# One pool of five PSUM banks in place of turns over pools of three and two, in a two-layer mixer trunk

## The chip, the cores and the metric

The kernel runs on one core of a Trainium2 chip. The metric is the device time of one launch in microseconds, as the median of three runs. Beside it stands one execution recorded by the hardware profiler; every duration below comes from that execution.

## What is computed

The reference runs two layers over 128 context tokens and 512 latent tokens that share all weights (model width 1024). Each layer is a half SwiGLU network, a token mixer, and a second half SwiGLU network:

```python
def trunk_layer(x, cond, lp, ssd_s0, ret_s0, ctx_kv):
    mod = (jax.nn.silu(cond) @ lp['w_mod'] + lp['b_mod'])[:, None, :]
...
    x = x + 0.5 * g1 * swiglu(modulate(rmsnorm(x, nw[0]), sh1, sc1), lp['ffn_w_in'][0], lp['ffn_w_out'][0])
    y, s_ssd, s_ret, k, v = token_mixing(modulate(rmsnorm(x, nw[1]), sh2, sc2), lp, ssd_s0, ret_s0, ctx_kv)
    x = x + g2 * y
    x = x + 0.5 * g3 * swiglu(modulate(rmsnorm(x, nw[2]), sh3, sc3), lp['ffn_w_in'][1], lp['ffn_w_out'][1])
```

Token mixing multiplies by one input matrix, gives the columns to four mixers (a state-space scan "ssd", a long convolution "hyena", a retention scan and a windowed attention), and multiplies what they return by one output matrix. The scans and the attention work in chunks of 128 tokens: five chunks, of which the first is the context. The hidden width of the SwiGLU networks is 2816.

## The kernel before

The 640 tokens are columns, held as two groups of 320. A large fp32 product is made of three TensorE products, of a high and a low part of each operand (`hh` and `hl` of the activations, `hi` and `lo` of the weights): high times high, high times low, low times high. In the rows these are `mm<-hh,hi`, `mm<-hh,lo` and `mm<-hl,hi`. They are called **large products** here. They use three PSUM banks (pool `mmp`, tile `mm`), and VectorE (DVE) or ScalarE (ACT) empties a bank when its sum is complete: gates of the mixers go through ACT (`u<-mm,ucg`), the mixers' output product is added to the residual on DVE (`x<-mm,gate,x`, in `accumulate`).

All the mixers' **small products** (scores, values, states, transposes by the identity `ident`) go through `mx()`, which hands out one bank of a second set of five. Before the change `mx()` counts its calls modulo five: turns 0 to 2 take a bank of pool `mxp` (three banks), turns 3 and 4 one of pool `xtp` (two banks). The turn belongs to the place of the call in the program text.

The second SwiGLU network of each layer (`ffn7`) replaces eight quarter products by seven (`quad`); there `mx()` keeps to the three banks (`self.wide = False`), and two of the results, `mb` and `mc`, take the two banks of `xtp`.

The engines work through their own instructions in order. That order isn't the one of the text: a scheduler lays the instructions of all streams out when the program is built, and takes an instruction when its engine and its tiles' buffers are free by its own reckoning. So large products of work that doesn't depend on a mixer are laid between that mixer's small ones, and which bank a tile waits for decides where. During a mixer the large products are those of the next mixer's inputs; the program's order of mixers is hyena, ssd, attention, retention, then the output product (`mix_out`).

In the attention (`attention`), for each chunk `scores` makes for each of four heads a tile `big` of up to 512 columns (two products: `mx<-u,u` and `mx<-ckT,u`) and, for chunks 1 to 3, a tile `right` of 128 columns, which DVE masks and reduces into `sc` (with the running maximum `amx`). ACT then takes the exponentials. `values` transposes `sc` on TensorE (`mx<-ident,sc`), copies to `pT`, and multiplies by the values (`mx<-u,pT`, `mx<-cv,pT`). In the retention (`retention`), `out1` of a chunk makes four score products (`mx<-u,u`, masked to `M`), for chunks after the first eight products with the states (`mx<-inc,u`, `mx<-st,u`), and four with the values (`mx<-u,M`); DVE and ACT normalise the result `y`, and `out2` transposes it one chunk later (`mx<-ident,y`) for `mix_out`. A small fp32 product stands in the trace with two instructions, a transpose with one.

A small product with `64*128` in its row of the trace contracts the 64 channels of a head, and its operands lie in partitions 0 to 63 or 64 to 127 (in the attention the lower half for heads 0 and 1, the upper for heads 2 and 3); the large products and the transposes contract 128.

The part of `scores` in which the tiles are asked for:

```python
                for h in range(4):
...
                    big = self.mx(512)
...
                    if hi > 512:
                        right = self.mx(128)
```

Of the kernel before, what the change touches and what calls it, by code (L numbers as in the profile page):

```python
# [10 lines left out]
F32 = mybir.dt.float32  # L11
# [4 lines left out]
PSUM = bass.MemoryType.PSUM  # L16
# [37 lines left out]
class Trunk:  # L54
# [38 lines left out]
        self.nc.tensor.transpose(out, in_, self.ident[b : b + n, b : b + n])  # L93

    def mx(self, *shape):

        self.turn = (self.turn + 1) % 5
        if self.wide and self.turn >= 3:
            t = self.xtp.tile([128, 512], F32, tag="xt", name="mx")
        else:  # L100
            t = self.mxp.tile([128, 512], F32, tag="mx", name="mx")
        return self.shaped(t, shape)

    @staticmethod
# [23 lines left out]
    def setup(self):  # L128
        tc, nc, ctx, I = self.tc, self.nc, self.ctx, self.I
        pool = lambda name, bufs=1, **k: ctx.enter_context(tc.tile_pool(name=name, bufs=bufs, **k))  # L130
        self.cp = cp = pool("const")
        self.sp = pool("small", 2)
        self.wp = pool("w", 3)
        self.ringp = pool("ring", NB)
        self.mmp = pool("mmp", 3, space=PSUM)
        self.xtp = pool("xtp", 2, space=PSUM)
        self.mxp = pool("mxp", 3, space=PSUM)
        self.turn, self.wide = 0, True
        self.ssum, self.V = {}, {}
        self.drp = pool("dr", 1, space=bass.MemoryType.DRAM)  # L140

        self.ident = cp.tile([128, 128], F32, name="ident")
        make_identity(nc, self.ident)
        self.ones = cp.tile([128, 128], F32, name="ones")
        nc.gpsimd.memset(self.ones, 1.0)
        self.mhalf = cp.tile([128, 8], F32, name="mhalf")
        nc.gpsimd.memset(self.mhalf, -0.5)
        self.sel = cp.tile([128, 2], F32, name="sel")
        self.dma(self.sel, I["sel"])
        cond = cp.tile([128, 8, 2], F32, name="cond")  # L150
        self.dma(cond, I["cond"])
        self.cs = self.ring("cs")[:, :256].rearrange("p (a b) -> p a b", a=8)
        nc.gpsimd.memset(self.cs, 0.0)
        self.act(self.cs[:, :, 0:2], cond, AF.Silu)
        self.par = []
        for li in range(NL):
            t = cp.tile([128, PC.n], F32, name=f"par{li}")
            self.dma(t, I["par"][li])
            self.par.append(t)
        self.xnew()  # L160

        self.hw = [[cp.tile([128, 8, 322 if g == 0 else 320], F32R, name=f"h{p}{g}") for g in range(2)] for p in "hl"]
        self.hh, self.hl = ([[self.hw[p][g][:, m, 0:320] for g in range(2)] for m in range(8)] for p in range(2))
        self.mod = [cp.tile([128, 72, 2], F32, name=f"mod{li}") for li in range(NL)]
        self.sc = [cp.tile([128, 3, 8, 2], F32, name=f"sc{li}") for li in range(NL)]
        self.gate = [cp.tile([128, 3, 8, 2], F32, name=f"gate{li}") for li in range(NL)]
# [326 lines left out]
    def quad(self, li, w, f, sp, mp, halves):  # L493

        nc = self.nc
        gate, up = (self.rawload(self.I["ffnin"][li, w, 2 * f + i], 1024) for i in range(2))
        a11, a12, a21, a22 = gate[:, :512], gate[:, 512:], up[:, :512], up[:, 512:]
        sa = sp.tile([128, 2, 512], F32, tag="sa", name="sa", bufs=1)  # L500
        sb = sp.tile([128, 2, 512], F32, tag="sb", name="sb", bufs=SB)
        add = self.tt
        ab = self.wsplit(gate)
        add(sa[:, 0], a21, a11, SUB)
        add(sb[:, 0], a21, a22, ADD)
        add(sa[:, 1], sb[:, 0], a11, SUB)
        add(sb[:, 1], a12, sa[:, 1], SUB)
        new = lambda pool, tag, name: pool.tile([128, 512], F32, tag=tag, name=name)[:, :320]
        A, B, C = new(self.mmp, "mm", "mm"), new(self.xtp, "xt", "mb"), new(self.xtp, "xt", "mc")
        sg = mp.tile([128, 640], F32, tag="sg", name="sg", bufs=2)  # L510

        def copied(ps, name):
            t = mp.tile([128, 320], F32, tag="cp", name=name, bufs=CB)
            self.acopy(t, ps)
            return t

        self.product(B, ab, 1, "B21", True, True)
        self.product(A, ab, 0, "B11", True, False)
        p1 = copied(A, "p1")
        self.tt(sg[:, :320], B, p1, ADD)  # L520
        self.act(sg[:, :320], sg[:, :320], AF.Silu)
        wa = self.wsplit(sa.rearrange("p a b -> p (a b)"))
        self.product(C, wa, 0, "T3", True, False)
        p7 = copied(C, "p7")
        yield
        w4 = self.wsplit(a22)
        self.product(A, wa, 1, "T2", False, False)
        q = copied(A, "q")
        self.product(C, w4, 0, "T4", False, True)
        self.tt(q, C, q, ADD)  # L530
        self.tt(sg[:, :320], q, sg[:, :320], MUL)
        gh = self.ring("gh", 640, F32R)
        gl = self.ring("gl", 640, F32R)
        if halves:
            self.split(gh[:, :320], gl[:, :320], sg[:, :320])
        yield
        wb = self.wsplit(sb.rearrange("p a b -> p (a b)"))
        self.product(A, wb, 0, "T1", False, False)
        self.tt(p7, A, p7, ADD)
        yield  # L540
        self.product(A, wb, 1, "B22", False, True)
        self.act(sg[:, 320:], A, AF.Silu)
        self.tt(sg[:, 320:], p7, sg[:, 320:], MUL)
        o = 320 if halves else 0
        self.split(gh[:, o:], gl[:, o:], sg[:, o:])
        self.G.append([(gh[:, 320 * g : 320 * g + 320], gl[:, 320 * g : 320 * g + 320]) for g in range(2)])

    def ffn7(self, li, w, todo, rate, after_group):
        I, n = self.I, 2 * w
        pool = lambda name: self.tc.tile_pool(name=name, bufs=2, side="right", reuse_waits="tile")  # L550
        with pool("ws") as sp, pool("ffn") as mp, pool("mods") as modp, self.tmp():
            self.wide = False
            mods = self.modulation(todo, modp, bufs=MBUF, pin=PIN) if todo else iter(())
            credit = 0.0
            self.G = []
# [76 lines left out]
                done = after_group(g)  # L632
                next(done, None)
            next(done, None)
            self.wide = True


    def sin(self, pool, a, ps, b, fr):
# [522 lines left out]
    def attention(self, li, UQ, UK, UV):  # L1161
        nc, I, O, pm = self.nc, self.I, self.O, self.par[li]
        Y = UQ
        with self.tc.tile_pool(name="att", bufs=1, side=SIDES["att"], reuse_waits="tile") as p:
# [53 lines left out]
            def scores(c):  # L1218
# [33 lines left out]
                if hi > 512:  # L1252
                    self.tt(mx, mx, mx2, MAX)
                self.tt(mx, mx, pm[:, PC.sink], MAX)
                neg = self.small([128, 4], "aneg")
                self.ts(neg, mx, -1.0, MUL)
                es = self.small([128, 4], "aes")
                self.tt(es, pm[:, PC.sink], neg, ADD)
# [398 lines left out]
```

## Time and profile before

| what | value |
| --- | --- |
| runs | 2802.38, 2803.92, 2805.83 us; median 2803.92 us |
| the profiled execution | 2796.57 us, of which the span from the first to the last instruction is 2794.8 us |
| TensorE (PE) busy | 2708.9 us, 97% of the span |
| VectorE (DVE) busy | 1921.8 us, 69% |
| ScalarE (ACT) busy | 1001.2 us, 36% |
| mean granted TensorE clock | 0.987 of full speed |

The profiled execution lies 7.35 us under the median of the runs. A busy engine is one with an instruction under way; on PE a busy microsecond can still be a slow one, as the granted clock of a stretch shows. An idle stretch on PE is named in the rows with the instruction that ended it.

### The profile page before, as it was taken

How to read it: one execution, taken by the hardware profiler on the slowest of the kernel's cores; microseconds unless marked ns; L12 is line 12 of the kernel's file. 1: busy time of each engine (PE TensorE's matmuls, PEld its weight loads, DVE VectorE, ACT ScalarE, POOL GpSimd, SP SyncE). 2: the span in 40 equal slices, each digit the busy share in tenths (PEclk: the TensorE clock that was granted, in tenths of full speed). 3: DMA queues.
4: the chain of work that ended last, by engine and by line, in shares of the span. 5: the costliest groups of instructions: out<-in, count | busy, mean ns of one | idle time of the engine just before them, and what ended most of it. 6: DMA issues, size and time to landing. Idle time of an engine off the chain costs nothing.

```text
span 2794.8 us, 45752 instructions
## 1 busy us (share of the span) xinstructions
PE 2708.9 (97%) x17990; PEld 2601.4 (93%) x17990; DVE 1921.8 (69%) x4040; ACT 1001.2 (36%) x2047; POOL 115.6 (4%) x191
## 2 busy tenths in 40 slices
PE   5999999999999999999999999999999999999999
PEld 3899999999889899999989999998999888999999
DVE  5867677666765688766677676676568467766666
ACT  3222222332544353333442223223336434334432
POOL 0000000100010200000020000002001002000000
PEclk9999999999999999999999999999999999999999
DMA  7454544421213123222235444443213021222222
GB/s 265 145 183 144 159 143 162 136 81 63 80 51 99 52 76 117 85 86 76 82 138 181 146 144 137 143 155 99 80 57 101 18 72 59 83 81 72 83 73 94
DMA packets 121169, 300.52 MB, mean 108 GB/s; under 512 B 20062, under 2 KB 44974, under 8 KB 120572
## 3 DMA queue, kind: packets, MB, share of 16 engines
q1 hardware_dynamic: 120956, 297.61, 33.1%
q8 instruction: 142, 2.33, 0.3%
q14 instruction: 71, 0.58, 0.1%
HBM read 283.36 MB, written 14.20 MB: 106 GB/s over the span
## 4 chain that ended last, share of the span: by engine, by line
PE 89%; DVE 5%; POOL 1%; issue 1%; ACT 1%; DMA 1%; SPq 0%; POOLq 0%; ACTq 0%; DVEq 0%
PE mm L88 70%; PE mx L88 10%; PE mc L88 5%; PE mb L88 3%; PE mx L93 2%; DVE lo L61 1%; DVE x L70 1%; POOL nsum L294 1%; ACT hi L76 0%; DMA E<-cumd 0%; DVE wmj L278 0%; DVE hl L61 0%; DVE nx L70 0%; DVE gl L61 0%; POOL nrs L125 0%
## 5 line engine op out<-in xcount | busy, mean ns | idle before, releaser
L88 PE MATMUL mm<-hh,hi 128*128 128x320 f32 (+2 forms) x3136 | 993.0, 317 | 9.1 <-ACT hh L76 4.0
L88 PE MATMUL mm<-hh,lo 128*128 128x320 f32 (+2 forms) x3136 | 989.5, 316 | 7.7 <-DVE lo L61 7.7
L88 PE MATMUL mm<-hl,hi 128*128 128x320 f32 (+2 forms) x3136 | 990.4, 316 | 2.1 <-DVE hl L61 2.1
L76 ACT CAST hi<-raw 128x1024 fp32r<-128x1024 f32 (+4 forms) x406 | 346.0, 852 | 858.1 <-PE mm L88 809.4
L88 PEld LDWEIGHTS mm<-hh,hi 128*128 128x128 f32 (+1 forms) x3136 | 596.6, 190 | 19.3 <-ACT hh L76 5.6
L88 PEld LDWEIGHTS mm<-hh,lo 128*128 128x128 f32 (+1 forms) x3136 | 598.9, 191 | 16.0 <-DVE lo L61 8.4
L88 PEld LDWEIGHTS mm<-hl,hi 128*128 128x128 f32 (+1 forms) x3136 | 597.1, 190 | 13.5 <-issue 5.6
L61 DVE TENSOR_TENSOR lo<-raw,hi 128x1024 fp32r<-128x1024 f32 (+4 forms) x406 | 395.5, 974 | 183.0 <-ACT hi L76 182.0
L88 PE MATMUL mm<-gh,hi 128*128 128x320 f32 x1408 | 437.5, 311 | 7.2 <-DVE x L70 6.7
L88 PE MATMUL mm<-gl,hi 128*128 128x320 f32 x1408 | 435.2, 309 | 1.8 <-DVE gl L61 1.4
L88 PE MATMUL mm<-gh,lo 128*128 128x320 f32 x1408 | 434.5, 309 | 0.0
L70 DVE SCALAR_TENSOR_TENSOR x<-mm,gate,x 128x128 f32<-128x128 f32 (+2 forms) x624 | 253.8, 434 | 181.1 <-PE mm L88 178.6
L278 DVE CUSTOM_DVE_ANT_0 wmj<-wm,condb 128x1024 bf16<-128x1024 f32 x264 | 321.2, 1217 | 2.4 <-ACT condb L73 1.2
L88 PEld LDWEIGHTS mm<-gh,hi 128*128 128x128 f32 x1408 | 264.3, 188 | 13.6 <-PE mm L88 9.7
L88 PEld LDWEIGHTS mm<-gl,hi 128*128 128x128 f32 x1408 | 264.4, 188 | 5.8 <-DVE gl L61 4.4
L88 PEld LDWEIGHTS mm<-gh,lo 128*128 128x128 f32 x1408 | 264.5, 188 | 0.0
L70 DVE SCALAR_TENSOR_TENSOR gu<-mm,cg,sg 128x128 f32<-128x128 f32 x132 | 54.2, 436 | 157.7 <-ACT cg L76 103.6
L294 POOL TENSOR_TENSOR nsum<-nsum,nsq 128x320 f32<-128x320 f32 x60 | 54.2, 904 | 1384.3 <-ACT nsq L73 946.6
L88 PE MATMUL mc<-th,lo 128*128 128x320 f32 x320 | 98.7, 309 | 0.1
L88 PE MATMUL mc<-th,hi 128*128 128x320 f32 x320 | 98.7, 308 | 0.0
L88 PE MATMUL mc<-tl,hi 128*128 128x320 f32 x320 | 98.6, 308 | 0.0
L76 ACT COPY cg<-mm 128x2 f32<-128x2 f32 x88 | 14.1, 160 | 213.6 <-PE mm L88 213.2
(283 smaller groups left out, 3247.6 us busy)
## 6 DMA issues: line engine op xcount, KB each, us to landing
raw<-in_ffnin SPq DMA_DIRECT2D x176, 512.0 KB, 3.5
wm<-in_wmodT SPq DMA_DIRECT2D x132, 512.0 KB, 3.6
raw<-in_mixin SPq DMA_DIRECT2D x52, 512.0 KB, 3.4
raw<-in_ffnoutA SPq DMA_DIRECT2D x80, 256.0 KB, 2.6
raw<-in_ffnoutA SPq DMA_DIRECT2D x48, 320.0 KB, 2.8
wms<-in_wmod SPq DMA_DIRECT2D x12, 512.0 KB, 3.4
raw<-in_ffnoutB SPq DMA_DIRECT2D x12, 512.0 KB, 3.4
raw<-in_mixout SPq DMA_DIRECT2D x16, 384.0 KB, 3.0
```

Source lines behind the costliest of these rows:

```text
L61: self.nc.vector.tensor_tensor(out, a, b, op=op)
L70: self.nc.vector.scalar_tensor_tensor(out, a, s, b, op0=op0, op1=op1)
L76: self.nc.scalar.copy(out, in_)
L88: return self.nc.tensor.matmul(out, lhsT=lhsT, rhs=rhs, start=start, stop=stop, **k)
L93: self.nc.tensor.transpose(out, in_, self.ident[b : b + n, b : b + n])
L278: return self.nc.vector.tensor_tensor_reduce(junk, raw, cb, 1.0, 0.0, op0=MUL, op1=ADD, accum_out=out)
L294: (adder or (self.nc.vector if g and m > 5 else self.nc.gpsimd)).tensor_tensor(s, s, sq, op=ADD)
```

## The change

`xtp` is taken away and `mxp` has five banks; `mx()` always takes the next bank of `mxp`, and so do `mb` and `mc`. The count of turns and the switch `wide` are gone. No arithmetic changes.

```diff
     def mx(self, *shape):
-
-        self.turn = (self.turn + 1) % 5
-        if self.wide and self.turn >= 3:
-            t = self.xtp.tile([128, 512], F32, tag="xt", name="mx")
-        else:
-            t = self.mxp.tile([128, 512], F32, tag="mx", name="mx")
+        t = self.mxp.tile([128, 512], F32, tag="mx", name="mx")
         return self.shaped(t, shape)
...
         self.mmp = pool("mmp", 3, space=PSUM)
-        self.xtp = pool("xtp", 2, space=PSUM)
-        self.mxp = pool("mxp", 3, space=PSUM)
-        self.turn, self.wide = 0, True
+        self.mxp = pool("mxp", 5, space=PSUM)
...
-        A, B, C = new(self.mmp, "mm", "mm"), new(self.xtp, "xt", "mb"), new(self.xtp, "xt", "mc")
+        A, B, C = new(self.mmp, "mm", "mm"), new(self.mxp, "mx", "mb"), new(self.mxp, "mx", "mc")
...
-            self.wide = False
...
-            self.wide = True
```

The scheduler lays out another order with it. TensorE's instructions are the same ones in both programs and stand in the same order in the SwiGLU networks; they stand elsewhere in the mixers of both layers, and a few at the start and around the norms. Three places follow, all of the first layer; the second layer's mixers show the same patterns.

First place, on TensorE (PE): the attention's scores of chunk 2. `u_7613` and `u_7610` are the keys, `u_7489`, `u_7551` and `u_7486`, `u_7548` the queries, `ckT` the cached keys. Before:

```order
L88 MATMUL mx<-u_7613,u_7489 128x256
L88 MATMUL mx<-ckT,u_7489 128x256
L88 MATMUL mm<-hh_106,lo 128x322
L88 MATMUL mm<-hh_106,hi 128x322
L88 MATMUL mx<-u_7613,u_7489 128x128
L88 MATMUL mx<-u_7613,u_7551 128x256
L88 MATMUL mx<-ckT,u_7551 128x256
L88 MATMUL mx<-u_7613,u_7551 128x128
L88 MATMUL mm<-hl_108,hi 128x322
```

And now:

```order
L88 MATMUL mx<-u_7610,u_7486 128x256
L88 MATMUL mx<-ckT,u_7486 128x256
L88 MATMUL mx<-u_7610,u_7486 128x128
L88 MATMUL mx<-u_7610,u_7548 128x256
L88 MATMUL mx<-ckT,u_7548 128x256
L88 MATMUL mx<-u_7610,u_7548 128x128
L93 MATMUL mx<-ident,sc 128x128 x4
L88 MATMUL mm<-hh_103,lo 128x322
```

The scores of a chunk (two such halves, eight tiles for chunks 1 to 3) now stand together, with transposes of the exponentials of the chunk before right behind them and no large product between; the large products follow in blocks of 2 to 23.

Second place, on TensorE: the end of the retention, from the last chunk's products with the values (`mx<-u,M`) to the transposes of the last two chunks of `y`; the large products are those of `mix_out`. Before:

```order
L88 MATMUL mx<-u_8615,M 128x64 x2
L88 MATMUL mx<-u_8677,M 128x64 x2
L93 MATMUL mx<-ident,y 128x128 x2
L88 MATMUL mm<-hh_107,hi 128x320
L88 MATMUL mm<-hl_109,hi 128x320
```

And now:

```order
L88 MATMUL mx<-u_8674,M 128x64 x2
L88 MATMUL mm<-hh_104,hi 128x320
L88 MATMUL mm<-hl_106,hi 128x320
L88 MATMUL mm<-hh_104,lo 128x320
...
L93 MATMUL mx<-ident,y 128x128 x2
L88 MATMUL mm<-hh_103,hi 128x320
```

Between the last `mx<-u,M` and the last but one `mx<-ident,y` there stand 12 large products now and none before (13 now in the second layer); between the two last `mx<-ident,y` 29 now and 14 before (36 and 14 in the second layer). They come from the blocks that stood between attention and retention (119 large products in the first layer, 81 in the second; 8 now in each) and behind the retention. Within the retention the products of one chunk stand together now, with 12 to 16 large ones to the next transposes.

Third place, on ScalarE (ACT): the end of the attention, where the retention's gate (`u_8736<-mm,ucg`, a silu) meets the last chunk's exponentials (`sc,asum<-sc,aneg`). Before, one load behind the whole attention served that gate. Now:

```order
L76 COPY ucg<-mm 128x2
L73 ACT_TABLE_LOAD
L73 ACTIVATE u_8736<-mm,ucg 128x128
...
L73 ACTIVATE u_8736<-mm,ucg 128x192
L76 COPY pT<-mx 128x128
L73 ACT_TABLE_LOAD
L73 ACTIVATE sc,asum<-sc,aneg 128x512 x4
L73 ACTIVATE aes<-aes 128x4
...
L73 ACT_TABLE_LOAD
L73 ACTIVATE u_8736<-mm,ucg 128x320
```

The gate's first half is now ahead of the exponentials and its second half behind them, so the function tables change three times where they changed once; over the program there are 13 table loads instead of 9, two more in each layer.

## Rows read from the trace of the kernel before

**Rows 1.** The page: span, and TensorE's busy time.

```profile
span 2794.8 us, 45752 instructions
...
PE 2708.9 (97%) x17990; PEld 2601.4 (93%) x17990; DVE 1921.8 (69%) x4040; ACT 1001.2 (36%) x2047; POOL 115.6 (4%) x191
```

**Rows 2.** The page: shares of the chain that ended last, by engine.

```profile
PE 89%; DVE 5%; POOL 1%; issue 1%; ACT 1%; DMA 1%; SPq 0%; POOLq 0%; ACTq 0%; DVEq 0%
```

**Rows 3.** The page: costliest groups, results of the seven products on TensorE.

```profile
L88 PE MATMUL mc<-th,hi 128*128 128x320 f32 x320 | 98.7, 308 | 0.0
```

**Rows 4.** Timeline of TensorE, end of retention: start, length, instruction, [idle before, releaser].

```profile
914.83 1.00 PE L88 MATMUL mx<-u,M 128*128 128x64 f32 x8
916.84 0.41 PE L93 MATMUL mx<-ident,y 128*128 128x128 f32 x2 [1.01 <-DVE y L61]
918.92 0.63 PE L88 MATMUL mm<-hh,hi 128*128 128x320 f32 x1 [1.66 <-DVE x L70]
...
2289.18 0.41 PE L93 MATMUL mx<-ident,y 128*128 128x128 f32 x2 [1.37 <-DVE y L61]
2291.25 0.63 PE L88 MATMUL mm<-hh,hi 128*128 128x320 f32 x1 [1.67 <-DVE x L70]
```

**Rows 5.** Timeline of DVE there, first layer.

```profile
916.27 0.43 DVE L61 TENSOR_TENSOR y<-y,rrr 128x256 f32<-128x256 f32 x1
...
916.95 0.34 DVE L70 SCALAR_TENSOR_TENSOR x<-mm,gate,x 128x128 f32<-128x128 f32 x1
...
918.46 0.87 DVE L70 SCALAR_TENSOR_TENSOR x<-mm,gate,x 128x192 f32<-128x192 f32 x2
```

**Rows 6.** Stretches (us): length, PE busy (instructions), granted clock, DMA share, GB/s.

```profile
2266.00:2273.00 7.00, 7.00 (x32) 0.52 0.01 2
...
918.90:924.90 6.00, 5.98 (x23) 0.50 0.20 66
924.90:930.00 5.10, 5.10 (x36) 1.00 0.32 103
...
2291.20:2297.10 5.90, 5.85 (x22) 0.51 0.19 51
```

**Rows 7.** The chain in order of time, first layer's ssd: start, length, what.

```profile
752.35 3.00 DMA E<-cumd
...
758.94 1.34 PE mx L88 x10
```

**Rows 8.** Waits of TensorE, 600 to 1000 us: total, times, longest.

```profile
PE mx L88 <- DVE E L61: 2.4, 1, 2.4
...
PE mx L88 <- DVE amx L1245: 0.3, 1, 0.3
```

**Rows 9.** Timeline of TensorE, first layer's attention, first scores of chunk 2.

```profile
812.94 0.70 PE L88 MATMUL mx<-u,u 64*128 64x256 f32 x2
813.48 0.38 PE L88 MATMUL mx<-ckT,u 64*128 64x256 f32 x1
813.53 0.48 PE L88 MATMUL mx<-u,u 64*128 64x256 f32 x1
```

**Rows 10.** The same timeline, the rest of three heads and large products around it.

```profile
814.59 0.41 PE L88 MATMUL mm<-hh,lo 128*128 128x322 f32 x1
814.84 0.31 PE L88 MATMUL mm<-hh,hi 128*128 128x322 f32 x1
815.08 0.92 PE L88 MATMUL mx<-u,u 64*128 64x128 f32 x4
...
816.58 0.41 PE L88 MATMUL mm<-hl,hi 128*128 128x322 f32 x1
816.83 0.31 PE L88 MATMUL mm<-hh,lo 128*128 128x322 f32 x1
816.98 0.31 PE L88 MATMUL mm<-hh,hi 128*128 128x322 f32 x1
```

**Rows 11.** Timeline of DVE there: the reductions of two successive heads.

```profile
814.11 0.69 DVE L1245 CUSTOM_DVE_ANT_0 sc<-mx,amask 128x512 f32<-128x512 f32 x1 [0.53 <-PE mx L88]
...
814.93 0.69 DVE L1245 CUSTOM_DVE_ANT_0 sc<-mx,amask 128x512 f32<-128x512 f32 x1
```

**Rows 12.** Timeline of ACT behind the attention: a table load and what follows.

```profile
865.47 1.28 ACT L73 ACT_TABLE_LOAD   x1
866.77 1.91 ACT L73 ACTIVATE condb<-condb 128x2048 f32<-128x2048 f32 x1
```

**Rows 13.** Timeline of DVE, retention: the same reduction of two successive chunks.

```profile
914.39 0.42 DVE L1138 TENSOR_REDUCE rvs<-vt 128x4 f32<-128x256 f32 x1
...
919.24 0.41 DVE L1138 TENSOR_REDUCE rvs<-vt 128x4 f32<-128x256 f32 x1
```

## The prediction

> **What bounds the kernel now.** I read the page first: TensorE is busy for 2708.9 of 2794.8 us [rows 1], and the chain that ended last runs over it for 89% [rows 2]. So what counts is TensorE's 86 us of idle time and its slow time; VectorE and ScalarE matter only where TensorE waits for them. The seven-product results have no wait ahead of them (0.0 us before `mc`, in 320 products [rows 3]), and their order stays, so I cost what the change does to `mb` and `mc` at nothing. Then I went through TensorE's timeline in both layers' mixers, looking for idle stretches and for the granted clock behind them.
>
> Three things are to be seen there. First, the end of the retention: when its last `mx<-u,M` is done (914.83 plus 1.00) there is no large product to do; TensorE stands 1.01 us for `y`, then 1.66 us for the additions to `x` that free the banks of the large products. The second layer does the same with 1.37 and 1.67 us [rows 4]. VectorE shows why: the addition at 916.95 stands behind the scaling of `y` at 916.27, and the next two only at 918.46 [rows 5]. Second, right behind either stall TensorE runs at half clock for some 6 us: 23 instructions fill 5.98 us there, while 36 fill 5.10 us in the stretch after it [rows 6]. Third, in the first layer's ssd the decay tile `E` is fetched by a 3.00 us transfer on the chain, and TensorE waits 2.4 us for what VectorE makes of it [rows 7, 8].
>
> **The change, part by part.** The arithmetic, TensorE's instructions and the number of banks stay. What changes is the order in which TensorE gets its small products, and four table loads on ScalarE.
>
> *The retention's end.* Twelve large products now stand between the last `mx<-u,M` and the transpose. One takes 5.10 us over 36, 0.142 us [rows 6], so twelve cover 1.7 us, more than the 1.01 and 1.37 us of the waits for `y`: 2.4 us gained. Behind the transpose 29 more (36 in the second layer) stand ahead of the next one, but the additions to `x` keep their place in VectorE's queue behind the chain of `y`, so I take only half of the waits for `x`: (1.66 + 1.67) / 2 = 1.7 us. Together 4.1 us gained; bounds 0, if the stall only moves behind the new blocks, and 5.7.
>
> *The clock behind it.* At 0.142 us each, the 23 and 22 instructions of the two slow stretches would take 3.3 and 3.1 us, not 5.98 and 5.85 [rows 6]: 2.7 + 2.7 = 5.4 us. Ahead of each slow stretch stood some 3 us of idle time within 5; with most of that filled I take the 5.4 us as gained. Bound: nothing, if what idle time is left keeps the clock low.
>
> *The ssd.* From the transfer's start to the next `mx<-u,E` it is 758.94 less 752.35, 6.6 us [rows 7]. Sixteen large products stood between these two chunks; 27 do now. Eleven more cover 1.6 us of the wait: 1.6 us gained, between 0 and the 2.4 us of the wait.
>
> *Fewer changes of shape.* Small products of 64 rows used to stand singly between large ones. A large product that is followed by one takes 815.08 less 814.84, 0.24 us, to its successor, where 816.98 less 816.83 is the usual 0.15 [rows 10]: some 0.09 us for a change from 128 to 64 rows, and I take the same for the way back. Counted along both orders there are 214 such changes before and 144 now: 70 x 0.09 = 6.3 us gained. Bounds: nothing, if the changes that go lie where TensorE then waits, and 9.5 us with the first large product behind a small one, which is slow as well (814.84 less 814.59, 0.25 us [rows 10]) in 35 excursions. I take the row's own price. The Trainium skill has the same direction without a time: "TensorEngine Tiling (Array Packing)", Key Properties, says that a change of tiling mode drains TensorE.
>
> *The scores, against it.* Eight tiles are now asked for in a row, with five banks. TensorE takes 1.65 us from 812.94 to 814.59 and 1.50 us from 815.08 to 816.58 for three heads [rows 9, 10], so 1.05 us a head; VectorE needs 814.93 less 814.11, 0.82 us, and starts 1.17 us after the first product [rows 9, 11]. So the first bank is free after 1.17 + 0.69 = 1.86 us, and TensorE asks for the sixth after two heads and a `big`, 2.7 us or more: no wait. What is lost is an overlap: two heads whose operands lie in different halves of the partitions ran at once (813.48 and 813.53, 0.05 us apart [rows 9], where 0.2 is usual); heads 0 and 1 share a half and now follow each other. At 0.16 us, twice in each of six chunks, it is at most 1.9 us; I take 1 us lost. Bounds: -0.3 us (the wait for `amx` that goes [rows 8]) and 4 us, if banks are still held by the chunk before and 0.3 us is waited in each chunk besides.
>
> *The table loads, against it.* Two more per layer at 1.28 us [rows 12]. Behind them on ScalarE stand the last chunk's exponentials, then copies to `pT`, for which TensorE's transposes and value products wait; 23 large products and the values of the chunk before are the cover. I take one load of two as seen: 1.3 us a layer, 2.6 us lost; bounds 0 and 5.1. The next instruction begins 866.77 less 865.47, 1.30 us, after the load [rows 12]: nothing else is lost by the row. The Trainium skill would have more: "ScalarE: Activation LUTs", What ACT_TABLE_LOAD costs, gives about 2.66 us for a switch with its drain, which would make the loss 5.3 us; the row decides.
>
> *The retention's chunks, against it.* Their products stand together now, while VectorE goes through a chunk in 4.85 us [rows 13]. TensorE's chunk is longer, with 12 to 16 large products (2 us), the eight instructions for the values (1.00 us [rows 4]) and 24 for scores and states at about as much each (3 us): 6 us, so no steady wait, but one for `M` or for a free bank may show. I take 0.5 us a layer, 1 us lost; bounds 0 and 3.
>
> **Sum.** -4.1 - 5.4 - 1.6 - 6.3 + 1 + 2.6 + 1 = -12.8 us, made against the profiled execution's 2796.57 us. The median of the runs lies 7.35 us above it; with the same gap after the change it is 2803.92 - 12.8, so **2791 us** (-0.46%). A measurement of this kernel can tell some 0.2% from no change, 5.6 us.
>
> **Rivals.**
> *No change that can be told.* As long as tiles are freed in the order in which they are asked for, the k-th tile takes the bank of the k-5th in either program, and waits may only move. If the changes of shape are worth nothing and the clock comes back in one layer only, the sum is -4.1 - 2.7 - 1.6 + 4.6 = -3.8: 2800 us. For it: all the idle time in the mixers is small, and the gain in clock needs nearly all of one stall to go. Against it: the waits for `y` [rows 4] have a cause in the order, and it is gone.
>
> *Slower: bunched small products pull TensorE's clock down.* Between 2266 and 2273 the clock is 0.52 with TensorE busy for all 7.00 us [rows 6]; no wait stands ahead of it, only small products of the retention with next to no large ones between. Now there are 14 such bunches (three chunks' scores and four of the retention's chunks, in each layer). A stretch of 7 us at half clock loses 3.5 us; with it behind six of them, +21 - 12.8 = +8.2: 2812 us. The time is slower by over 0.2% from 18.4 / 3.5, more than five of the 14. Against it: the scores of chunk 2 stood together for 1.65 us without it, and the wait that ended in them was 0.3 us [rows 8]. The Trainium skill speaks for it ("TensorE: Matmul & The Clock Gate", A second HAM failure mode: psum-queue depth-cycling): short idle times between groups that cycle through PSUM banks make the clock swing. No row shows that in the attention yet.
>
> *A larger gain.* Both stalls go whole (5.7 us), and bunches and loads cost nothing: -5.7 - 5.4 - 1.6 - 6.3 = -19.0, 2785 us.
>
> **How the numbers follow.** My sum's case, -6 to -17 us, has 0.48; the larger gain 0.14; no change 0.24; slower 0.14. So faster by over 0.2% has 0.62, within it 0.24, slower 0.14. The range goes from the larger gain with the shapes' upper bound in part (another 3 or 4 us, 2781) to 2807, between no change and the slow rival: outside lie about 0.05 below and 0.12 above. The likeliest case alone has 2787 to 2798.
>
> **What would show it.** Right: waits for `y` and `x` behind the retention's last `mx<-u,M` of under 2 us in either layer and a clock of 1.00 in the 6 us after it; no waits for `amx` of over 0.5 us a layer; two more loads in each attention, with the transposes of the last chunk late by a microsecond. Wrong: a half clock within the attention or the retention (the slow rival), a wait for `x` that only moves behind the new blocks (no change), or idle stretches in the SwiGLU networks, where I expect none.

## The result and the profile after

The changed kernel takes 2773.69 us (2773.55 to 2774.48), the kernel before 2803.15 us over the same runs: 29.5 us less, a ratio of 0.9897 with an interval of 0.9882 to 0.9913. I had forecast 2791 us, 12.8 us less, and a range that ends at 2781. The way was right, the size was less than half of what came.

The profiled execution of the changed kernel took 2774.48 us, of which the span is 2772.7 us. Against the 2796.57 us of before that is 22.1 us. The rest of the 29.5 us is in the runs: the profiled execution of before lies 6.6 us under the 2803.15 us (7.35 us under the median that I was shown), and that of after lies 0.8 us above its own. To carry that gap over to the changed kernel was wrong by itself.

The page of after, span and busy time, where [rows 1] stood:

```profile
span 2772.7 us, 45720 instructions
...
PE 2691.3 (97%) x17990; PEld 2593.6 (94%) x17990; DVE 1921.5 (69%) x4040; ACT 1006.2 (36%) x2051; POOL 113.5 (4%) x191
```

VectorE and ScalarE have the same work (four table loads more on ScalarE). TensorE has the same 17990 instructions in 17.6 us less of busy time, so most of the 22.1 us isn't idle time at all. To find it I took the two traces' stretches with the same 1600 or so TensorE instructions, from ahead of the first layer's ssd to its output product and the same in the second layer. First before, then after (length, TensorE busy and its instructions, granted clock, DMA share, GB/s):

```profile
703.00:943.50 240.50, 229.48 (x1606) 0.98 0.23 73
2079.50:2318.00 238.50, 232.20 (x1608) 0.97 0.22 67
```

```profile
710.50:931.00 220.50, 216.39 (x1606) 1.00 0.25 80
2074.00:2296.00 222.00, 217.07 (x1605) 1.00 0.22 71
```

Three things are to be seen. The mixers got 20.0 and 16.5 us shorter, 36.5 together, more than the whole gain of the trace, so some 14 us were lost elsewhere. The clock reads 1.00 now. And TensorE is busy for 28 us less with the same instructions.

The retention's end, where [rows 4] stood (TensorE's timeline):

```profile
913.54 0.78 PE L88 MATMUL mx<-u,M 128*128 128x64 f32 x6
914.13 0.39 PE L88 MATMUL mm<-hh,hi 128*128 128x320 f32 x1
...
915.99 0.38 PE L93 MATMUL mx<-ident,y 128*128 128x128 f32 x2
916.13 0.39 PE L88 MATMUL mm<-hh,hi 128*128 128x320 f32 x1
...
921.23 0.41 PE L93 MATMUL mx<-ident,y 128*128 128x128 f32 x2 [0.59 <-DVE y L61]
...
2276.50 0.38 PE L93 MATMUL mx<-ident,y 128*128 128x128 f32 x2
...
2283.76 0.44 PE L93 MATMUL mx<-ident,y 128*128 128x128 f32 x2 [0.66 <-DVE y L61]
```

In both layers there is no wait from the last `mx<-u,M` through the last but one transpose (915.99 and 2276.50) to the output product, where [rows 4] had 1.01 to 1.67 us. A shorter wait for `y` stands ahead of the last transpose instead, 0.59 and 0.66 us, where there was none before. No wait for `x` is left at either place. Behind it the clock stays whole, where [rows 6] showed 0.50:

```profile
873.00:925.00 52.00, 51.41 (x418) 1.00 0.31 103
...
2240.00:2286.00 46.00, 44.85 (x365) 1.00 0.16 49
```

TensorE's waits from 600 to 1000 us, where [rows 8] had 2.4 us for `E` and 0.3 us for `amx`:

```profile
PE mx L93 <- DVE q L61: 1.8, 1, 1.8
...
PE mm L88 <- DVE lo L61: 0.7, 1, 0.7
...
PE mx L88 <- DVE E L61: 0.4, 1, 0.4
```

There is no wait for `amx`, and within the attention the wait for `q` is the only one (1.8 us, where it was 1.2 us before). What I hadn't looked for stands in the retention. TensorE's timeline, first before and then after:

```profile
909.91 0.71 PE L88 MATMUL mx<-u,u 64*128 64x128 f32 x4
910.54 0.41 PE L88 MATMUL mm<-hh,hi 128*128 128x320 f32 x1
```

```profile
910.51 0.72 PE L88 MATMUL mx<-u,u 64*128 64x128 f32 x8
911.05 0.33 PE L88 MATMUL mx<-inc,u 64*128 64x64 f32 x2
```

Before, four instructions took 0.63 us to the next one's start; now eight take 0.54 us. Before, the starts were 0.21, 0.11, 0.11 and 0.20 us apart, and the first and the last of these are longer because the shape changes there. Now they start in pairs: 0.01 us apart within a pair, 0.20 us to the second pair and 0.10 us to the later ones. By the program's text these are score products of heads whose operands lie in different halves of the partitions, and where such products are neighbours, they run at once; the last experiment tests this. The Trainium skill states it ("TensorEngine Tiling (Array Packing)", Key Properties: different tiles can execute in parallel); the trace agrees with eight in 0.54 us. The order with large products in between had kept them apart.

### The profile page after: what moved, and what is told of

Read it like the earlier page. It is cut to its first block, busy times and chain, and to the rows that moved or that the text cites. A ratio compares the mean times of both kernels' runs of the same rounds, so it can differ in the third digit from the quotient of the medians.

```text
span 2772.7 us, 45720 instructions
## 1 busy us (share of the span) xinstructions
PE 2691.3 (97%) x17990; PEld 2593.6 (94%) x17990; DVE 1921.5 (69%) x4040; ACT 1006.2 (36%) x2051; POOL 113.5 (4%) x191
## 4 chain that ended last, share of the span: by engine, by line
PE 90%; DVE 5%; ACT 1%; POOL 1%; issue 1%; DMA 1%; SPq 0%; POOLq 0%; DVEq 0%; ACTq 0%
PE mm L88 70%; PE mx L88 10%; PE mc L88 5%; PE mb L88 3%; PE mx L93 2%; DVE lo L61 1%; DVE x L70 1%; POOL nsum L287 1%; ACT hi L76 0%; DVE wmj L271 0%; DVE gl L61 0%; DVE hl L61 0%; POOL nrs L120 0%; ACT gh L76 0%; DVE nsum L287 0%
## 5 line engine op out<-in xcount | busy, mean ns | idle before, releaser
L88 PEld LDWEIGHTS mm<-hl,hi 128*128 128x128 f32 (+1 forms) x3136 | 595.0, 190 | 12.3 <-issue 5.2
L76 ACT COPY cg<-mm 128x2 f32<-128x2 f32 x88 | 14.1, 160 | 213.5 <-PE mm L88 213.3
```

The lines of the kernel that those rows point to most:

```text
L76: self.nc.scalar.copy(out, in_)
L88: return self.nc.tensor.matmul(out, lhsT=lhsT, rhs=rhs, start=start, stop=stop, **k)
```

## The experiments

Each table row below is worked out from a trace, by adding up the times from one start of TensorE to the next over two stretches of 1600 instructions (the 4350th to the 5950th and the 13300th to the 14900th by their start, the stretches shown above). Low clock is the time, without the idle time, that the clock column gives as half speed; half of it is lost. The last column is the sum less that half, so the time as it would be at full clock.

| kernel | both stretches, us | of it idle | at low clock | at full clock |
| --- | --- | --- | --- | --- |
| before | 477.6 | 17.3 | 21.9 | 466.6 |
| the change | 441.4 | 9.0 | 0 | 441.4 |
| five in the ssd | 468.4 | 15.0 | 9.9 | 463.5 |
| five in the attention | 473.1 | 17.6 | 37.1 | 454.6 |
| five in the retention | 460.2 | 13.2 | 3.4 | 458.4 |
| five in ssd and attention | 459.7 | 13.3 | 18.6 | 450.4 |
| five in ssd and retention | 456.2 | 10.2 | 3.4 | 454.5 |
| five in all three | 442.2 | 9.8 | 0 | 442.2 |
| turns from 1 | 458.8 | 10.1 | 0 | 458.8 |
| turns from 3 | 467.7 | 13.3 | 9.4 | 463.1 |
| five in the rest only | 479.7 | 15.8 | 29.3 | 465.0 |
| all three, halves alternating | 437.3 | 11.5 | 0 | 437.3 |

**One mixer at a time.** The theory was that each mixer's new order is worth what the two traces' stages differ by; the rival, that the mixers share the large products and the parts don't add. The two sets of banks are closed and opened again at the edges of a mixer's program text. Outside the two stretches of the table, each trace of these kernels has TensorE's instructions in the order of before, one for one.

```diff
-        if self.wide and self.turn >= 3:
+        if self.wide and not self.five and self.turn >= 3:
...
+    def banks(self, five):
+        if five == self.five:
+            return
+        self.five = five
+        self.bst.close()
+        pool = lambda name, n: self.bst.enter_context(
+            self.tc.tile_pool(name=name, bufs=n, space=PSUM, reuse_waits="tile"))
+        if five:
+            self.mxp = pool("mxp", 5)
+        else:
+            self.xtp = pool("xtp", 2)
+            self.mxp = pool("mxp", 3)
...
         for name in ORDER:
+            self.banks(name in ('att',))
```

The ssd alone. Expected:

> Pool of five only while the ssd's program text runs, turns of three and two everywhere else. Theory (each mixer's new order is worth what the stages of the two traces differ by: the ssd -8.0 us in the first layer, +1.2 in the second): about -7 us against before. Rival (the parts hang together through the large products that they share, so one part alone moves its wait to the next mixer): within 3 us of before.

Measured: 2797.45 us, ratio 0.9987 (0.9978 to 0.9996), 3.6 us by the ratio; the interval, 1 to 6 us, lies short of the theory's 7 and partly within the rival's 3. The attention alone. Expected:

> Pool of five only in the attention. Theory (additive): the stages of the traces differ by -3.9 and -7.0 us, so about -11 us. Rival (shared large products): the attention takes large products that the retention's end needs; -3 us or less, with the stalls for y and x at the retention's end as long as before or longer. My prediction's own terms (changes of shape gained, a table load lost) would give -2 us.

Measured: 2795.21 us, ratio 0.9982 (0.9970 to 0.9994), 5 us, between the theory and the rival. The retention alone. Expected:

> Pool of five only in the retention. Theory (additive): -8.2 and -11.8 us, so about -20 us, with both stalls at the retention's end and the half clock behind them gone. Rival (shared large products): the block between attention and retention stays, so the same or more, -20 to -25. If the end's stall needs the attention's order as well: -5 us and the stalls still there.

Measured: 2788.92 us, ratio 0.9959 (0.9947 to 0.9971), some 11.5 us, about half of what either of the first two expected. Its trace has neither the stalls at the retention's end nor the half clock behind them, so the end doesn't need the attention's order. All three. Expected:

> Pool of five in ssd, attention and retention; turns in hyena, filters, norms and the seven-product networks. Theory (the gain comes from these three mixers; 4.1 us are lost at the start and 3 us around each of two norms in the traces): as fast as the full change or up to 5 us faster, 2769 to 2775 us. Rival (the networks' mb and mc or the hyena carry a part): slower than the full change by over 3 us.

Measured: 2765.39 us, ratio 0.9876 (0.9863 to 0.9888): 35 us, more than either expected, and by the ratios (0.9876 against 0.9897, whose intervals just touch) some 6 us less than the full change takes. Three parts of 3.6, 5 and 11.5 us give 20, not 35; so as sums of times they don't add, and the theory falls in that form. The last column of the table says why: at full clock the parts are worth 3.1, 12.0 and 8.2 us, together 23.3, and all three 24.4.

That is one execution of each kernel, and in these the stretches themselves give 9.2, 4.5 and 17.4 us, 31.1 together against 35.4. The runs carry it further. The time of each run multiplied by its granted clock, averaged over a kernel's runs, falls by 0.7, 11.8 and 7.3 us in the three parts (19.8 together) and by 22.1 us with all three, each known to some 2 us (the ssd's may be up to 4.5 us too small, as its trace lacks the clock of the start; the last section has more on that). The rest of the time is what the low clock costs, and it changes by -3.5, +6.6 and -5.4 us (-2.3 together), but by -14.0 us with all three. So what doesn't add is the clock. The attention alone runs longer at low clock than before. Its second layer (stretches of TensorE, then two waits):

```profile
2181.00:2188.00 7.00, 7.00 (x33) 0.52 0.01 2
...
2266.60:2280.30 13.70, 13.70 (x59) 0.50 0.00 1
...
2290.50:2300.70 10.20, 7.83 (x30) 0.50 0.07 12
```

```profile
2293.24 0.66 PE L93 MATMUL mx<-ident,y 128*128 128x128 f32 x2 [0.94 <-DVE y L61]
2295.33 0.63 PE L88 MATMUL mm<-hh,hi 128*128 128x320 f32 x1 [1.43 <-DVE x L70]
```

The first stretch is in the bunched scores themselves, behind a wait of 1.19 us for `q`: what my slow rival expected, in one attention of one run. The other two are in the retention, which still has its turns, its stalls and its slow stretches there. Two more kernels test this, the pairs with and without the retention:

> Pool of five in the ssd and the attention, turns in the retention and everywhere else: the fourth run without the retention. The first three runs gave -3, -5 and -12 us, together -20, where the fourth gave -35. If the parts add and the 15 us between are the clock in the retention: -8 us, with the stalls at the retention's end and a low clock there. If the 15 us come from attention and ssd together, whatever the retention does: -20 to -25 us.

Measured: 2782.88 us, ratio 0.9934 (0.9908 to 0.9960), with the stalls (1.37 and 1.67 us) and three slow stretches in the retentions. This is 18.5 us by the ratio and 22.2 us by the medians. The interval, 11 to 26 us, leaves out the 8 us of the first expectation and holds the second, though the stalls and the low clock of the first are there. At full clock it is 16.2 us in the table, where the two parts give 15.1.

> Pool of five in the ssd and the retention, turns in the attention. If what the attention gives alone is hidden by the clock that falls in the retention behind it (so that with the retention mended it is worth its full 15 to 20 us): -15 us, and no low clock in the mixers. If the attention is worth 5 us in any company: -30 us.

Measured: 2783.29 us, ratio 0.9928 (0.9915 to 0.9942), some 20 us and between the two expectations, with 3.4 us of low clock in the mixers; at full clock 12.1 us, where the parts give 11.3. With the attention added it becomes 24.4 us at full clock, 12.3 more: the attention is worth some 12 to 13 us at full clock in each company tried, and the clock hides it when it comes alone.

**Another draw of turns.** Is it the pool, or is any other order as good? The kernel before with its count of turns started elsewhere:

```diff
-        self.turn, self.wide = 0, True
+        self.turn, self.wide = 1, True
```

> The kernel before with its count of turns started at 1 instead of 0, so that every small tile is bound to the other pool by another phase. Theory (fixed turns as such break the order up, whichever phase they have): 2795 to 2806 us, stalls at other places, and as many changes between 64 and 128 rows. Rival (the phase of before is a bad draw, and the gain is that another order was drawn): under 2788 us.

Measured: 2788.12 us, ratio 0.9943 (0.9924 to 0.9962), 13.5 us less: outside the theory's range, and at the rival's bound.

> The same with the count started at 3. Theory: 2795 to 2806 us again. Rival (luck of the draw): under 2788 us, or far from the phase started at 1, by over 10 us.

Measured: 2797.14 us, ratio 0.9981 (0.9970 to 0.9992), 4.5 us less: within the theory's range, and 9 us from the other phase. So luck of the draw is part of it. Started at 1, the turns happen to leave large products at the retention's end. TensorE's stretches in the mixers, and its one wait for `x` from 600 to 1000 us:

```profile
711.00:941.50 230.50, 225.66 (x1607) 1.00 0.24 76
2078.50:2308.00 229.50, 224.28 (x1606) 1.00 0.22 69
```

```profile
PE mm L88 <- DVE x L70: 0.2, 1, 0.2
```

The clock is whole, and the idle time in the mixers is 10.1 us, near the pool's 9.0 and not the 17.3 of before. But TensorE is still busy for 225.7 and 224.3 us, where the pool has 216.4 and 217.1 with the same number of instructions. Both phases keep as many changes between 64 and 128 rows as before (106 and 108 in the two stretches, against 110 before and 40 with the pool). So of the mixers' 36.2 us, 18.8 come with a draw that has no such stall, and the other 17.4 with the pool and with none of the three draws that ran (two phases weren't run).

**The rest of the program.** The opposite of the fourth kernel; `mb` and `mc` share the five banks here.

```diff
-            self.banks(name in ('ssd', 'att', 'ret'))
+            self.banks(name not in ('ssd', 'att', 'ret'))
...
-        A, B, C = new(self.mmp, "mm", "mm"), new(self.xtp, "xt", "mb"), new(self.xtp, "xt", "mc")
+        A, B, C = new(self.mmp, "mm", "mm"), new(self.mxp, "mx", "mb"), new(self.mxp, "mx", "mc")
```

> The opposite of the fourth run: pool of five at the start, in the filters, the hyena, the norms and the seven-product networks (mb and mc too), turns in ssd, attention and retention. Theory (the full change loses some 8 us there, as the two traces and the fourth run say): +8 us, 2806 to 2810 us, with 3 us lost in the first 65 us. Rival (the 8 us are where the clock happens to fall): within 3 us of before.

Measured: 2808.35 us, ratio 1.0028 (1.0016 to 1.0040), 6.7 us more, as the theory said. The start is the clearest part of it. Rows from there, and the first large product of the program, first before and then in the full change:

```profile
44.90 1.50 PE L88 MATMUL mx<-wms,cs 128*32 128x256 f32 x22
...
50.74 0.77 PE L88 MATMUL mx<-sel,modrow 128*128 128x2 f32 x4 [1.53 <-ACT modrow L76]
54.26 1.01 PE L88 MATMUL mx<-sel,modrow 128*128 128x2 f32 x4 [0.55 <-ACT modrow L76]
55.76 0.91 PE L88 MATMUL mm<-hh,hi 128*128 128x322 f32 x2 [0.49 <-ACT hh L76]
```

```profile
45.24 1.93 PE L88 MATMUL mx<-wms,cs 128*32 128x256 f32 x16
...
57.92 1.01 PE L88 MATMUL mx<-sel,modrow 128*128 128x2 f32 x4 [0.55 <-ACT modrow L76]
59.42 0.91 PE L88 MATMUL mm<-hh,hi 128*128 128x322 f32 x2 [0.49 <-ACT hh L76]
```

The products of the modulation (`mx<-wms,cs`) alternate in eights with the small ones that wait for their copy on ScalarE; before, more of them stood together, and TensorE waited three times instead of six. These waits differ little in sum (2.6 us before, 3.1 us now). The pace differs more: 22 products in 1.43 us to the next start before, 16 in 1.93 us now, so about half. The first large product comes 3.7 us later; in this run it comes at 59.56, as in the full change. The order alone isn't shown to cost all of that. In the nine traces that have the order of before at the start, the first large product comes at 55.6 to 58.2 us; in the three with five banks there it comes at 59.4 to 59.6. So by these traces some 1.3 us at least go with the order; the rest differs from execution to execution.

**Halves side by side.** If neighbouring 64-row products in different halves run at once, then ordering them so must gain more. The fourth kernel (five in all three mixers) with another order of the same products:

```diff
-                for h in range(4):
+                for h in (0, 2, 1, 3):
                     kv = h // 2
...
-                for e in range(2):
-                    pS = self.mx(2, 128)
-                    for pr in range(2):
-                        self.mm(pS[:, pr], UK[pr][64 * e : 64 * e + 64, o : o + 128], UQ[pr][64 * e : 64 * e + 64, o : o + 128])
-                    self.tt(M[:, :, e], pS, Dv[:, :, e], MUL)
+                pS = [self.mx(2, 128) for e in range(2)]
+                for pr in range(2):
+                    for e in range(2):
+                        self.mm(pS[e][:, pr], UK[pr][64 * e : 64 * e + 64, o : o + 128], UQ[pr][64 * e : 64 * e + 64, o : o + 128])
+                for e in range(2):
+                    self.tt(M[:, :, e], pS[e], Dv[:, :, e], MUL)
```

The products with the states (`pn`) are turned in the same way.

> The fourth run with the score products of the attention ordered by head 0, 2, 1, 3 and those of the retention alternating between the two halves of the partitions. Theory (neighbouring 64-row products in different halves run at once, and the change gained by bringing them together): the products between 64-row ones go from 113 ns to 60 to 80 ns apart, -6 to -15 us against the fourth run (2750 to 2760 us). Rival (what the change gained there is only fewer changes of shape): no difference beyond 3 us.

Measured: 2762.13 us, ratio 0.9857 (0.9835 to 0.9880), against 0.9876 of the fourth kernel: some 5 us, between the two expectations, and the intervals overlap. The traces are clearer: 437.3 us in the mixers against 442.2, and the time from one 64-row instruction's start to the next falls from 113 to 92 ns (380 in the two stretches), less than expected. The retention's products with the states, 16 instructions, take 0.93 us now (903.79 to 904.72):

```profile
903.79 0.34 PE L88 MATMUL mx<-inc,u 64*128 64x64 f32 x4
903.96 0.39 PE L88 MATMUL mx<-st,u 64*128 64x64 f32 x4
904.18 0.39 PE L88 MATMUL mx<-inc,u 64*128 64x64 f32 x4
904.40 0.39 PE L88 MATMUL mx<-st,u 64*128 64x64 f32 x4
904.72 0.42 PE L88 MATMUL mm<-hl,hi 128*128 128x320 f32 x1
```

In the full change the same 16 take 1.44 us, from the 911.05 shown above to the large product at 912.49. So neighbours in different halves do run at once, and the rival falls. This is the fastest kernel here; it ran once more beside the full change on one chip:

> The eighth kernel again, beside the full change on one chip. It keeps turns outside the three mixers (the traces: 7 us less than the full change, of which the start and the norms give 3 each) and alternates halves (5 us by the mixers' part of its trace): 11 to 12 us faster than the full change, 2761 to 2764 us. Rival (the differences outside the mixers are the state of the chip): 5 us.

> The full change again on the same chip: 2772 to 2776 us, ratio to before 0.988 to 0.991.

Measured: 2764.70 us (ratio 0.9858, 0.9842 to 0.9874) and 2772.43 us (0.9894, 0.9875 to 0.9912): 7.7 us between them, not 11 to 12 and not 5. In the mixers the two traces differ by 5.5 us, which leaves some 2 us outside them.

## Why the prediction was right in direction and wrong in size

The bound was read rightly: TensorE's waits and its slow time in the mixers. In the trace, step by step:

*The retention's end and the ssd.* I gave 4.1 and 1.6 us of waits back. All the idle time in the mixers fell by 8.3 us. The halving of the waits for `x` was too careful: they went whole. The waits for `y` were to go whole and moved in part behind the new block: 2.4 us before, 1.25 after. The wait for `E` fell from 2.4 to 0.4 us in the first layer, but one of 0.7 us is new in the second.

*The clock behind it.* Forecast 5.4 us, for two slow stretches. All 21.9 us of low clock in the mixers went, which is 11.0 us. The mechanism was right; I had left out the other two stretches, of which the one from 2266 us [rows 6] stood among my rows, and I used it only as the slow rival's argument.

*Fewer changes of shape, the scores and the retention's chunks.* This is the step that failed. I took 70 changes at 0.09 us, 6.3 us, and gave 2 us back for the scores and the chunks. Without idle time and at full clock the mixers' work takes 449.3 us before (477.6 less 17.3 and 11.0) and 432.4 us after: 16.9 us gained, not 4.3. The count of changes was right (110 to 40 in the two stretches). The price of one was too small: 16.9 us over 70 are 0.24 us each, and the kernels in between lie near that line (the attention alone loses 50 changes and 12.4 us of this work, the retention alone 22 changes and 4.1).

The rows show why. At a change my 0.09 us holds, in either direction: in the stretches before, at full clock and without idle time, the median from a large product's start to the next large one's is 0.148 us and to a 64-row product's 0.238, and from a 64-row product of 128 columns to its like it is 0.111 and to a product of 128 rows 0.202. But the product behind the change is slow as well, and on both sides: the first large product behind a 64-row one takes 0.252 us to the next, the first 64-row one behind a large one 0.213, some 0.10 us more than usual (0.05 for the shorter small products). I had this in [rows 10] for the large side, and kept it for the upper bound only. With it a change costs 0.14 to 0.19 us, which makes some 12 us of the 16.9, an estimate from these medians and the counts.

The loss of overlap had the wrong sign besides. Of the neighbouring 64-row products, 78 of 345 started within 0.06 us of each other before and 120 of 380 do now: 60 became 96 in the retention, and the attention, where I expected the loss from one pair of rows ([rows 9]), went from 18 to 24. What the pairs gave of the 16.9 us isn't separated; the last order of halves shows that pairing can be worth 6.6 us more with the same changes (437.3 less 11.5, against 442.2 less 9.8).

*The table loads.* Forecast 2.6 us lost; the loads are there, and TensorE's one wait in each attention is for `q`, which VectorE ends. ScalarE's timeline in the full change, with the load ahead of the gate's second half:

```profile
856.64 0.88 ACT L76 COPY pT<-mx 128x512 f32<-128x512 f32 x3
857.54 1.28 ACT L73 ACT_TABLE_LOAD   x1
858.84 0.53 ACT L73 ACTIVATE u<-mm,ucg 128x320 f32<-128x320 f32 x1
861.57 0.75 ACT L76 COPY pT<-mx 128x512 f32<-128x512 f32 x2 [2.21 <-PE mx L93]
```

ScalarE then waits 2.21 us itself: this load lies in its slack. It starts 0.02 us after the copy ends, and the next instruction starts 1.30 us behind its start, as in [rows 12]; the 2.66 us of the Trainium skill ("ScalarE: Activation LUTs", What ACT_TABLE_LOAD costs) don't show here either.

*What I had at nothing.* The seven products' results cost nothing, as I said: the order is the same, and before and after `mc` waits for 0.0 to 0.2 us. But outside the mixers the profiled execution of after lost 14.1 us, and the kernel with the pool there alone lost 6.7 us. I had seen in the orders that a few instructions move at the start and didn't price them: a term put at nothing without a reason. Some 7 us of the 14.1 are the low clock behind the start, mostly around the norms: 51.2 us at half clock against 36.6 before. Traces with the order of before there have 38.8 to 49.0 us, so that part isn't laid to the change.

The sum, for the 16.7 us between -12.8 and -29.5: the gap of execution and median 7.4, waits 2.6, clock 5.6, work 12.6, loads 2.6, and 14.1 the other way. That the forecast missed by 16.7 us and not by nearly twice as much is luck: the 14.1 us hid a part of it.

Of the rivals, "no change" fell: the waits didn't only move, and the changes of shape were worth more than nothing. That the order differs because a tile of one pool takes whichever bank is free is read from the program; no run tests it. The slow rival's stretch came in the attention of one kernel, at one place. The larger gain came nearer with the waits (7.3 us of 8.3), but it had the same price for a change.

## What to carry to other kernels

Tiles bound to pools by a fixed count fix, by accident, which product stands beside which. A common pool lets a scheduler keep products of one shape together, and here that is worth nearly as much (16.9 us) as all the waits and the clock that it takes away (19.3 us); so count neighbours and shapes in the new order, not only waits, and price a change of shape with the product behind it. Before pricing a reorder by parts, take the clock out: here the parts add at full clock and not in measured time. A pool can be right in one stage and wrong in another: the kernel with it in the three mixers alone is 35 us faster than before, the one with it everywhere else 6.7 us slower.

## What the hardware showed unexpectedly

A kernel's parts were worth 3.1, 12.0 and 8.2 us at full clock, but 3.6, 5 and 11.5 us in time, as the clock fell elsewhere: 37.1 us at half clock in the mixers with the pool in the attention alone, none with it in all three.

The clock column counts time without a clock record as whole. In the full change the trace holds no record before 63.2 us, and the column gives 1.00 from 0 to 65 us, while the large products there start 0.27 us apart (60.13, 60.40, 60.66), as they do at half clock elsewhere; they come to 0.15 us at 63.3. The trace of before has records from 44.2 us on and shows the half clock, from 51.0 to 61.2 us. So the spacing of like products is to be read beside the column.

```profile
0.00:65.00 65.00, 35.28 (x175) 1.00 0.67 239
```

```profile
60.13 0.47 PE L88 MATMUL mm<-hl,hi 128*128 128x322 f32 x1
60.40 0.47 PE L88 MATMUL mm<-hh,lo 128*128 128x322 f32 x1
60.66 0.47 PE L88 MATMUL mm<-hh,hi 128*128 128x322 f32 x1
```
